# An encoder layer on one core: the last three down projections computed with 128 tokens on the output's partitions, and the Fourier projection's weights placed 192 bytes further in their slots

## The chip, the core and the metric

The kernel runs on one core of one Trainium2 chip. The metric is device time in microseconds for one call, the median of several runs. A profile of one execution goes with it: every instruction of each engine with its start and duration, and every DMA.

The engines are named as in the profile: PE (TensorE, products), PEld (its loading of the stationary operand), DVE (VectorE), ACT (ScalarE), POOL (GpSimd) and SP, which issues most DMAs.

## The reference

One layer of an encoder on 512 tokens with 1024 features, all in fp32:

```python
def reference(x, ...):
    x = x + 0.5 * swiglu(rms_norm(x, ffn1_norm), ffn1_w_gate, ffn1_w_up, ffn1_w_down)
    h = rms_norm(x, mix_norm)
    u = h @ w_in
    f_out = fourier_mixer(u[..., :o0], fnet_w, fnet_b)       # 512 columns
    a_out = gqa_attention(u[..., o0:o1], u[..., o1:o2], u[..., o2:], q_norm, k_norm)
    x = x + jnp.concatenate([f_out, a_out], axis=-1) @ w_out
    x = x + 0.5 * swiglu(rms_norm(x, ffn2_norm), ffn2_w_gate, ffn2_w_up, ffn2_w_down)
    return rms_norm(x, final_norm)

def swiglu(h, w_gate, w_up, w_down):
    return (jax.nn.silu(h @ w_gate) * (h @ w_up)) @ w_down
def rms_norm(x, g):
    return x * lax.rsqrt(jnp.mean(x * x, axis=-1, keepdims=True) + EPS) * g
```

The hidden width of the two feed-forward parts is 2752: 21 blocks of 128 and a tail of 64.

## The kernel before

The state `x` lies transposed: eight blocks `x[k]` (k = 0 to 7) of 128 features on the partitions and 512 tokens along the free axis. Every operand of a product is split into a high and a low part (fp32r), and each product is made as three: high weights with high data, high weights with low data, low weights with high data (`product`, lines 160 to 163).

**The ring.** `ring` holds twelve slots of 4096 bytes per partition. The first eight (`own`) hold the scaled state in high and low parts (`hh`, `hl`) while a projection reads it, and otherwise weights; the other four (`plain`, slots 8 to 11, in pairs of a high and a low one) hold weights. Between the large tiles stand small unused ones (`room`), which set how far apart the addresses of a product's two operands are. SKIP puts the weights of the last three down projections 64 bytes further in their slots.

**Feed-forward.** The 21 hidden blocks go in groups, the last of them 14 to 20. In a group, `seven` makes the gate and up projections of each block by a scheme of seven half-size products (L389, 256 columns, tiles p, q and r), and `down` adds the group's share of the down projection to each of the eight feature blocks (L160 to L163, tile dn, 512 columns). `rest` is the piece of `seven` that stands behind the first of these. The first products of such a run are cut in two (CUT).

**The mixers** run by an order written out by hand (ORDER). There the Fourier projection (`fproject_ops`, L940 to L942) makes 8 blocks of 24 products with 256 columns: the scaled state in the ring is the stationary operand, the weights f0 to f3, in pairs of plain slots or in the tile `more`, are the moving one.

**The end.** In the second feed-forward part the last three feature blocks (5, 6, 7) are left to `closing`. It scales the first five blocks by the final gain (`gained`), then makes the three down projections for tokens 0 to 255, block after block, and then again for tokens 256 to 511. Each adds to the state (`residual`, L476), is squared (`square`, L194) and added to the sum of squares `acc`. In the middle of the second half the norm of the first half is worked out (`column`: sums over the partitions by products with ones, L216; `mean`, L223; `power`, L230, on POOL), turned into a row (`turn`, L235) and multiplied on the first half's output (`finish`, L1282 on DVE and L1278 on POOL), which goes out. After the last product the same follows for tokens 256 to 511. `awake` makes products without use, so that PE is not idle meanwhile.

PE and SP execute in the order of the program in both feed-forward parts. There, DVE, ACT and POOL get an order by what is ready first, worked out when the program is built.

Of the kernel before, what the change touches and what calls it, by code (L numbers as in the profile page):

```python
# [13 lines left out]
P = 128  # L14
S = 512
# [6 lines left out]
HD = 64  # L22
EPS = 1e-6
WARM = 9
NS = 12

GROUPS1 = ((0, "t", 1, 2), range(3, 9), range(9, 15), range(15, 21))
# [47 lines left out]
def asf(ap):  # L75
    return ap.bitcast(F32)
# [3 lines left out]
def encoder(ctx, tc, A, out):  # L80
    nc = tc.nc
    cp = ctx.enter_context(tc.tile_pool(name="const", bufs=1))
    wp = ctx.enter_context(tc.tile_pool(name="weights", bufs=3))
    ring = cp.tile([P, NS, KD * P], F32R, name="ring")
    taken = []

    def room(pool, n):
# [10 lines left out]
    def bank(name):  # L98
        return pp.tile([P, S], F32, tag="bank", name=name)
# [6 lines left out]
    hh = [ring[:, k, 0:S] for k in range(KD)]  # L106
    hl = [ring[:, k, S:] for k in range(KD)]


    def in_order():  # L110
# [6 lines left out]
    def lows(lo, src, hi):  # L117
        nc.vector.tensor_tensor(out=lo, in0=src, in1=asf(hi), op=ALU.subtract)  # L118

    slots = [ring[:, i, :] for i in range(NS)]  # L120
    plain = slots[KD:]

    def slot():
# [22 lines left out]
    def weights(src, name, n=KD, raw=None, by_dma=False, skip=0):  # L146
        raw = raw or raw_tile(src, name, n)
        hi, lo = weight_slots(n, skip)
        if name in HI_DVE:
            nc.vector.tensor_copy(hi[:, :n, :], raw[:, :n, :])  # L150
        else:
            nc.scalar.copy(hi[:, :n, :], raw[:, :n, :])  # L152
# [103 lines left out]
    def ffn(norm, after, wgu, wd, wdt, groups, opening, closing):  # L256
# [6 lines left out]
        with tc.tile_pool(name=f"act{n_}", bufs=1) as ap, tc.tile_pool(name=f"sums{n_}", bufs=2) as sp:  # L263
# [4 lines left out]
            wt = []  # L268
            free, where = list(range(PLACES)), {}

            def place(j):
# [1 line left out]
                return where[j]  # L273

            own, shared = slots[:KD], slots[KD:]

            def gate(c, between={}, by_dma=False):
                whi, wlo = weights(wgu[c], f"gu{n_}_{c}", by_dma=by_dma)
# [175 lines left out]
            def down(d, group, gi):  # L454

                js = [j for j in group if j != "t"]
                whi, wlo = weights(wd[d][:, js[0] : js[-1] + 1, :], f"dn{n_}_{d}_{gi}", len(js), skip=SKIP if closing and gi == len(groups) - 1 and d >= KD - 3 else 0)
                w = wt[d // 4][:, d % 4 * P : (d % 4 + 1) * P]

                def steps(ps, t):  # L460
                    for i, j in enumerate(group):
                        h, l = (at[:, where[j], o, t] for o in range(2))
                        first, last = i == 0, i == len(group) - 1
                        if j == "t":
                            nc.tensor.matmul(ps[:, t], w, h, start=first, stop=False)
                            nc.tensor.matmul(ps[:, t], w, l, start=False, stop=last)
                        else:
                            k = j - js[0]
                            cut = first and d == KD - 3 and t == slice(0, HALF)
# [3 lines left out]
                return steps  # L473

            def residual(d, ps, t):
                nc.vector.scalar_tensor_tensor(  # L476
# [4 lines left out]
            for gi, group in enumerate(groups):  # L481
# [34 lines left out]

                waiting, downs = [], []
                for d in range(KD):
                    if last and closing and d == KD - 3:
                        closing([(e, down(e, group, gi)) for e in range(d, KD)], residual)  # L520
# [24 lines left out]
                    waiting = []  # L545
# [133 lines left out]
    with tc.tile_pool(name="mix", bufs=1) as mp, tc.tile_pool(name="mixt", bufs=1) as mt:  # L679

        room(mp, 192)
        more = mp.tile([P, 2, KD * P], F32R, name="more")
        more = [more[:, i, :] for i in range(2)]
        plain.extend(more)

        def temp(name):
# [40 lines left out]
        def weight_ops(name, src, n=KD):  # L727
            @op(f"{name}.r")
            def _():
                raws[name] = raw_tile(src, name, n)  # L730

            @op(f"{name}.h")
            def _():
                ws[name] = hi, lo = tuple(weight_slots())
                (nc.vector.tensor_copy if name in HI_DVE else nc.scalar.copy)(hi[:, :n, :], raws[name][:, :n, :])
# [531 lines left out]

    by_pool = (2, 3)

    def finish(c0, c1, row, parts):  # L1270

        t = slice(c0 * P, c1 * P)
        pr = row(c0, c1)
        for ks in parts:
            block = slice(ks[0], ks[-1] + 1)
            if ks[0] in by_pool:
                for k in ks:
                    nc.gpsimd.tensor_tensor(out=x[k][:, t], in0=x[k][:, t], in1=n3.rb[:, t], op=ALU.mult)  # L1278
                    nc.scalar.dma_start(out=out[:, k, t], in_=x[k][:, t])
            else:  # L1280
                y = xt[:, block, t]
                nc.vector.tensor_tensor(out=y, in0=y, in1=pr[:, t].unsqueeze(1).to_broadcast(list(y.shape)), op=ALU.mult)  # L1282
                nc.sync.dma_start(out=out[:, block, t], in_=y)

    def gained(k, t=slice(0, S)):
        nc.scalar.activation(x[k][:, t], x[k][:, t], AF.Copy, scale=gains[:, 3, k : k + 1])
# [5 lines left out]
        for _ in range(2 * n):  # L1292
            nc.tensor.matmul(ps[:, : 2 * P], unit[:, :P], unit, start=True, stop=True)

    def closing(downs, residual):

        for k in range(downs[0][0]):
            gained(k)
        t0, t1 = slice(0, S // 2), slice(S // 2, S)

        def more(sq, t):
            nc.vector.tensor_tensor(out=n3.acc[:, t], in0=n3.acc[:, t], in1=sq[:, t], op=ALU.add)

        for d, steps in downs:
            ps = bank(f"last{d}0")
            for _ in steps(ps, t0):
                pass
            residual(d, ps, t0)
            more(n3.square(d, t0), t0)
            gained(d, t0)  # L1310
        i = 0
        for d, steps in downs:
            ps = bank(f"last{d}1")
            for _ in steps(ps, t1):
                i += 1
                if i == 5:
                    n3.column([n3.acc], 0, 2)
                if i == 9:
                    finish(0, 2, n3.row, ((0, 1), (4, 5), (2, 3), (6, 7)))
            if d < KD - 1:  # L1320
                residual(d, ps, t1)
                sq = n3.square(d, t1)
                if d == downs[0][0]:
                    more(sq, t1)
                gained(d, t1)

        pc = bank("ss3_2")
        for c in (2, 3):
            n3.sum(pc, c, [n3.acc], first=c == 2, last=False, skip_group_check=True)
        awake(1)  # L1330
        for c in (2, 3):
            n3.sum(pc, c, [sq], first=False, last=False, skip_group_check=True)
        residual(KD - 1, ps, t1)
        sq = n3.square(KD - 1, t1)
        gained(KD - 1, t1)
        for c in (2, 3):
            n3.sum(pc, c, [sq], first=False, last=c == 3, skip_group_check=True)
        awake(2)
        n3.mean(pc, 2, 4)
        n3.power(2, 4)  # L1340
        finish(2, 4, n3.rows, ((0,), (1,), (4, 5), (2, 3), (6, 7)))
# [50 lines left out]
def _layout(i):  # L1392
# [13 lines left out]
    def down(w):  # L1406
# [27 lines left out]
        "wdt1": i["ffn1_w_down"][NF * P :],  # L1434
        "wdt2": i["ffn2_w_down"][NF * P :],
        "wins": chunks(w_in[:, np.concatenate([k, q, v])]),
        "winf": w_in[:, :512].reshape(2, 4, P, 2, 256).transpose(3, 0, 2, 1, 4).reshape(4, P, 4, 256),
        "wo": chunks(i["w_out"][mix]),
    }
# [21 lines left out]
```

## Time and profile before

| what | value |
|---|---|
| median of 3 runs | 841.4 us (841.1 to 841.55) |
| the profiled execution | 841.31 us, span 839.5 us |
| PE busy | 831.3 us, 5433 products |
| DVE, ACT, POOL busy | 637.6, 463.7, 31.7 us |
| DMA | 84.0 MB read, 2.1 MB written |

The span is the time from the first to the last instruction that the profiler records; the rest of the execution's time lies around it. Products are pipelined: what a product costs is the distance between its start and the next one's start, not its own duration. In a row of the timeline stand the start, the duration, the engine, the line, the operation and the tiles (output, arrow, inputs), the shape and the count. In a row of the groups stand the count, the busy time and the mean duration in ns, and behind the next bar the idle time ahead of the group with the engine that ended it.

### The profile page before, as it was taken

How to read it: one execution, taken by the hardware profiler on the slowest of the kernel's cores; microseconds unless marked ns; L12 is line 12 of the kernel's file. 1: busy time of each engine (PE TensorE's matmuls, PEld its weight loads, DVE VectorE, ACT ScalarE, POOL GpSimd, SP SyncE). 2: the span in 40 equal slices, each digit the busy share in tenths (PEclk: the TensorE clock that was granted, in tenths of full speed). 3: DMA queues.
4: the chain of work that ended last, by engine and by line, in shares of the span. 5: the costliest groups of instructions: out<-in, count | busy, mean ns of one | idle time of the engine just before them, and what ended most of it. 6: DMA issues, size and time to landing. Idle time of an engine off the chain costs nothing.

```text
span 839.5 us, 13715 instructions
## 1 busy us (share of the span) xinstructions
PE 831.3 (99%) x5433; PEld 753.4 (90%) x5433; DVE 637.6 (76%) x1003; ACT 463.7 (55%) x777; POOL 31.7 (4%) x35
## 2 busy tenths in 40 slices
PE   9999999999999999999999999999999999999996
PEld 6888998899989998889998888899988998899986
DVE  6998896489746847699998388999945896489553
ACT  7763664167424744677776357656632673167452
POOL 0110000000000000221000000100000000000002
PEclk9999999999999999999999999999999999999999
DMA  7664322323242213522020224543233322323213
GB/s 251 171 149 164 126 89 76 119 101 138 77 137 101 70 47 112 189 84 75 26 76 26 85 90 114 119 160 118 93 117 110 133 89 77 119 101 100 70 58 101
DMA packets 31568, 89.38 MB, mean 106 GB/s; under 512 B 3728, under 2 KB 9360, under 8 KB 31504
## 3 DMA queue, kind: packets, MB, share of 16 engines
q1 hardware_dynamic: 28320, 82.87, 29.3%
q0 software_dynamic: 2608, 5.12, 3.3%
q8 instruction: 42, 0.69, 0.3%
q10 hardware_dynamic: 576, 0.52, 0.2%
q14 instruction: 22, 0.18, 0.1%
HBM read 84.04 MB, written 2.10 MB: 103 GB/s over the span
## 4 chain that ended last, share of the span: by engine, by line
PE 99%; POOL 0%; issue 0%; POOLq 0%; DVE 0%
PE r L389 23%; PE q L389 11%; PE dn L160 9%; PE dn L163 9%; PE dn L162 9%; PE p L389 6%; PE mix L160 3%; PE mix L162 3%; PE mix L163 3%; PE gu L640 3%; PE gu L160 3%; PE gu L163 3%; PE gu L162 3%; PE mix L1145 2%; PE mix L1102 2%; PE mix L1076 1%
## 5 line engine op out<-in xcount | busy, mean ns | idle before, releaser
L389 PE MATMUL r<-rt,ring 128*128 128x256 f32 x1686 | 209.7, 276 | 0.0
L389 PEld LDWEIGHTS r<-rt,ring 128*128 128x128 f32 x1686 | 200.7, 188 | 0.9
L162 PE MATMUL dn<-at,ring 128*128 128x512 f32 x300 | 116.7, 389 | 0.0
L163 PE MATMUL dn<-at,ring 128*128 128x512 f32 x300 | 116.7, 389 | 0.0
L160 PE MATMUL dn<-at,ring 128*128 128x512 f32 x300 | 116.7, 389 | 0.0
L389 PE MATMUL q<-rt,ring 128*128 128x256 f32 x840 | 106.7, 276 | 0.0
L118 DVE TENSOR_TENSOR ring<-s,ring 128x1024 fp32r<-128x1024 f32 x70 | 85.5, 1221 | 24.3 <-ACT ring L348 20.9
L476 DVE SCALAR_TENSOR_TENSOR gx<-dn,gx 128x512 f32<-128x512 f32 x61 | 42.0, 689 | 80.6 <-PE dn L163 80.6
L389 PEld LDWEIGHTS q<-rt,ring 128*128 128x128 f32 x840 | 100.5, 188 | 0.0
L152 ACT CAST ring<-raw_dn 128x768 fp32r<-128x768 f32 (+3 forms) x58 | 45.5, 788 | 82.9 <-PE dn L162 74.7
L348 ACT CAST ring<-s 128x1024 fp32r<-128x1024 f32 x70 | 73.5, 1050 | 28.7 <-PE p L389 15.0
L163 PEld LDWEIGHTS dn<-at,ring 128*128 128x128 f32 x300 | 56.3, 188 | 11.8
L162 PEld LDWEIGHTS dn<-at,ring 128*128 128x128 f32 x300 | 56.3, 188 | 11.3
L160 PEld LDWEIGHTS dn<-at,ring 128*128 128x128 f32 x300 | 56.3, 188 | 11.2
L118 DVE TENSOR_TENSOR ring<-raw_dn,ring 128x768 fp32r<-128x768 f32 (+3 forms) x58 | 51.6, 892 | 5.9 <-PE r L389 4.6
L389 PE MATMUL p<-rt,ring 128*128 128x256 f32 x420 | 53.3, 276 | 0.0
L118 DVE TENSOR_TENSOR ring<-raw_g,ring 128x1024 fp32r<-128x1024 f32 x35 | 42.7, 1219 | 10.3 <-PE p L389 10.3
L389 PEld LDWEIGHTS p<-rt,ring 128*128 128x128 f32 x420 | 50.2, 188 | 0.0
L348 ACT CAST ring<-raw_g 128x1024 fp32r<-128x1024 f32 x35 | 36.8, 1052 | 14.5 <-DMA raw_g<-in_wgu 8.8
L397 ACT COPY p<-r 128x256 f32<-128x256 f32 x35 | 12.9, 369 | 49.0 <-PE r L389 48.7
L421 ACT ACTIVATE g<-g 128x512 f32<-128x512 f32 x35 | 22.2, 633 | 23.4 <-DVE g L420 23.2
L357 ACT CAST ring<-raw_u 128x512 fp32r<-128x512 f32 x35 | 21.8, 624 | 17.0 <-PE q L389 16.2
(307 smaller groups left out, 1570.4 us busy)
## 6 DMA issues: line engine op xcount, KB each, us to landing
raw_g<-in_wgu SPq DMA_DIRECT2D x35, 512.0 KB, 3.6
raw_u<-in_wgu SPq DMA_DIRECT2D x35, 512.0 KB, 4.3
raw_dn<-in_wd SPq DMA_DIRECT2D x40, 384.0 KB, 3.1
raw_gu<-in_wgu SPq DMA_DIRECT2D x12, 512.0 KB, 3.6
raw_o<-in_wo SPq DMA_DIRECT2D x8, 512.0 KB, 3.5
raw_dn<-in_wd SPq DMA_DIRECT2D x8, 448.0 KB, 3.2
raw_wq<-in_wins SPq DMA_DIRECT2D x4, 512.0 KB, 4.4
raw_f<-in_winf SPq DMA_DIRECT2D x4, 512.0 KB, 4.0
```

The costliest lines, as they stand in the source:

```text
L118: nc.vector.tensor_tensor(out=lo, in0=src, in1=asf(hi), op=ALU.subtract)
L152: nc.scalar.copy(hi[:, :n, :], raw[:, :n, :])
L160: nc.tensor.matmul(ps, whi, mhi, start=first, stop=False)
L162: nc.tensor.matmul(ps[:, t], whi, mlo[:, t], start=False, stop=False)
L163: nc.tensor.matmul(ps, wlo, mhi, start=False, stop=last)
L348: nc.scalar.copy(hi, src)
L357: nc.scalar.copy(hi, src)
L389: nc.tensor.matmul(ps[:, t], a[:, ks], b[:, i, t], start=first and i == 0 and o == 0, stop=i == KH - 1 and o == 2, skip_group_check=not first,
L421: nc.scalar.activation(b["g"], b["g"], AF.Silu)
L476: nc.vector.scalar_tensor_tensor(out=x[d][:, t], in0=ps[:, t], scalar=0.5, in1=x[d][:, t], op0=ALU.mult, op1=ALU.add)
L640: nc.tensor.matmul(pss[c], w[:, k % 2, c], m[k], start=k == 0 and m is hh and w is hi, stop=k == KD - 1 and w is lo,)
L1102: nc.tensor.transpose(pts[n][:, c * P : (c + 1) * P], prob[t, b, c][:, kc * P : (kc + 1) * P], ident)
```

## The change

**The end.** The products of tokens 0 to 255 stay. For tokens 256 to 511, the three blocks of features are no longer made one after the other. `token_weights` makes a second copy of the three down projections' weights, times 0.5, in two tiles `tw` (high and low) laid out as 384 features beside each other, in slots 0 to 5. `by_tokens` then takes 128 tokens at a time: it turns the state's three blocks into the bank by three transposes, and adds 21 products with the hidden data as the stationary operand and 384 feature columns as the moving one. The bank holds tokens on the partitions, state already included, so the residual, its square and its gain are not separate steps. `inverse` squares the bank with a sum along the free axis and adds it to the rest of the mean square. `finish` scales these 384 features by the token's factor and a broadcast gain row `gt`, loaded from memory, and the other five blocks by the turned row, and sends 128 tokens out at a time. The first of the two groups of tokens is finished while the second is made, after 12 of its 21 products.

**The output's layout** changes to one piece for each half, put in order on the host.

**The mixers.** The pairs of slots that hold f0 to f3 are used 192 bytes (48 elements) further (`further`). For that, 256 bytes are left between slots 9 and 10 and behind slot 11, and behind the second slot of `more`. Slots 10 and 11 stand 256 bytes further in the whole kernel.

```diff
+FURTHER = 48
+FURTHER_IN = "f0", "f1", "f2", "f3"
+ROOM = 64
+LAST = 3
...
-    ring = cp.tile([P, NS, KD * P], F32R, name="ring")
+    ring = cp.tile([P, NS * KD * P + 2 * ROOM], F32R, name="ring")
...
-    slots = [ring[:, i, :] for i in range(NS)]
+    def slot_at(tile, i, rooms=0):
+        o = i * KD * P + rooms * ROOM
+        return tile[:, o : o + KD * P]
+
+    slots = [slot_at(ring, i, int(i >= KD + 2)) for i in range(NS)]
+
+    def further(tile, i, rooms=0):
+        o = i * KD * P + rooms * ROOM + FURTHER
+        return tuple(tile[:, o + j * KD * P : o + (j + 1) * KD * P].rearrange("p (a b) -> p a b", b=P) for j in range(2))
...
+            def token_weights(d, group):
+                c = slice((d - KD + LAST) * P, (d - KD + LAST + 1) * P)
+                hi, lo = (t[:, : len(group), c] for t in tw)
+                raw = raws[d][:, : len(group)]
+                nc.scalar.activation(hi, raw, AF.Copy, scale=0.5)
+                nc.vector.scalar_tensor_tensor(
+                    out=lo, in0=raw, scalar=0.5, in1=asf(hi), op0=ALU.mult, op1=ALU.subtract
+                )
+
+            def by_tokens(ps, c, group):
+                t = slice(c * P, (c + 1) * P)
+                for i in range(LAST):
+                    nc.tensor.matmul(
+                        ps[:, i * P : (i + 1) * P], x[KD - LAST + i][:, t], ident, is_transpose=True,
+                        start=i == 0, stop=False, skip_group_check=True,
+                    )
+                for j in group:
+                    h, l = (at[:, where[j], o, t] for o in range(2))
+                    whi, wlo = (w[:, j - group[0]] for w in tw)
+                    for a, b in ((h, whi), (l, whi), (h, wlo)):
+                        nc.tensor.matmul(
+                            ps[:, : LAST * P], a, b, start=False, stop=j == group[-1] and b is wlo, skip_group_check=True
+                        )
+                    yield
...
-    def closing(downs, residual):
+    def closing(downs, residual, by_tokens, finished):
...
+        gt = tp.tile([P, S], F32, tag="wide", bufs=1, name="gt")[:, :n]
+        nc.sync.dma_start(out=gt, in_=A["gt"])
...
+        def inverse(c, ps, z=None):
+            sq = tp.tile([P, S], F32, tag="sq", name=f"sqt{c}")
+            cs = slice(c, c + 1)
+            nc.scalar.activation(sq[:, :n], ps[:, :n], AF.Square, scale=D**-0.5, accum_out=squares[:, cs])
+            if c == 3:
+                sums = bank("ss3_3")
+                n3.sum(sums, c, [n3.acc])
+                n3.mean(sums, c, c + 1)
+            nc.vector.tensor_tensor(out=squares[:, cs], in0=squares[:, cs], in1=n3.ms[:, cs], op=ALU.add)
+            nc.gpsimd.tensor_tensor(out=n3.r[:, cs], in0=squares[:, cs], in1=mhalf[:, cs], op=ALU.pow)
+            if c == 3:
+                nc.vector.tensor_tensor(out=z, in0=ps[:, :n], in1=gt, op=ALU.mult)
+
+        def finish(c, ps, last):
+            t = slice(c * P, (c + 1) * P)
+            pr = bank(f"rp3_{c}")
+            n3.turn(pr, c)
+            y = finished(c)
+            r = n3.r[:, c : c + 1]
+            if last:
+                nc.scalar.activation(y[:, :n], z, AF.Copy, scale=r)
+                nc.scalar.dma_start(out=rest[:, c - 2, :n], in_=y[:, :n])
+            else:
+                nc.vector.scalar_tensor_tensor(out=y[:, :n], in0=ps[:, :n], scalar=r, in1=gt, op0=ALU.mult, op1=ALU.mult)
+            for a, b, how in ((0, 3, nc.sync), (3, fewer, nc.scalar)) if last else ((0, fewer, nc.sync),):
+                o = y[:, n + a * P : n + b * P]
+                row = pr[:, t].unsqueeze(1).to_broadcast([P, b - a, P])
+                nc.vector.tensor_tensor(out=o.rearrange("p (k s) -> p k s", s=P), in0=xt[:, a:b, t], in1=row, op=ALU.mult)
...
+        for c in (2, 3):
+            ps = bank(f"last{c}")
+            for i, _ in enumerate(by_tokens(ps, c)):
+                if (c, i) == (2, 2):
                     n3.column([n3.acc], 0, 2)
+                    sums = bank("ss3_2")
+                    n3.sum(sums, 2, [n3.acc])
+                    n3.mean(sums, 2, 3)
+                if (c, i) == (2, 5):
+                    finish_half()
+                if (c, i) == (3, 3):
+                    finish(*done[-1], False)
+            inverse(c, ps, z)
+            done.append((c, ps))
+        awake(4)
+        finish(*done[-1], True)
```

More of the change, by code (lines that the diff above doesn't have):

```diff
@@ L105, in encoder @@
     x = [xt[:, k, :] for k in range(KD)]
-    hh = [ring[:, k, 0:S] for k in range(KD)]
-    hl = [ring[:, k, S:] for k in range(KD)]
+    hh = [ring[:, k * KD * P : k * KD * P + S] for k in range(KD)]
+    hl = [ring[:, k * KD * P + S : (k + 1) * KD * P] for k in range(KD)]
     def in_order():
@@ L275, in ffn @@
             own, shared = slots[:KD], slots[KD:]
+            tw = [
+                ring[:, 3 * i * KD * P : 3 * i * KD * P + PLACES * LAST * P]
+                .rearrange("p (m c) -> p m c", c=LAST * P) for i in range(2)
+            ]
             def gate(c, between={}, by_dma=False):
@@ L456, in down @@
                 js = [j for j in group if j != "t"]
-                whi, wlo = weights(wd[d][:, js[0] : js[-1] + 1, :], f"dn{n_}_{d}_{gi}", len(js), skip=SKIP if closing and gi == len(groups) - 1 and d >= KD - 3 else 0)
+                src, halves_ = wd[d][:, js[0] : js[-1] + 1, :], closing and gi == len(groups) - 1 and d >= KD - LAST
+                raw = raws[d] = raw_tile(src, f"dn{n_}_{d}_{gi}", len(js))
+                whi, wlo = weights(src, "", len(js), raw, skip=SKIP if halves_ else 0)
+                if halves_:
+                    token_weights(d, js)
                 w = wt[d // 4][:, d % 4 * P : (d % 4 + 1) * P]
@@ L518, in ffn @@
                 for d in range(KD):
-                    if last and closing and d == KD - 3:
-                        closing([(e, down(e, group, gi)) for e in range(d, KD)], residual)
+                    if last and closing and d == KD - LAST:
+                        closing(
+                            [(e, down(e, group, gi)) for e in range(d, KD)], residual,
+                            lambda ps, c: by_tokens(ps, c, group), finished,
+                        )
                         break
@@ L681, in encoder @@
         room(mp, 192)
-        more = mp.tile([P, 2, KD * P], F32R, name="more")
-        more = [more[:, i, :] for i in range(2)]
+        more_tile = mp.tile([P, 2 * KD * P + ROOM], F32R, name="more")
+        more = [slot_at(more_tile, i) for i in range(2)]
         plain.extend(more)
@@ L734, in _ @@
                 ws[name] = hi, lo = tuple(weight_slots())
+                if name in FURTHER_IN:
+                    i = next(i for i, t in enumerate([slots[KD], slots[KD + 2], more[0]]) if t is plain[-2])
+                    assert plain[-1] is [slots[KD + 1], slots[KD + 3], more[1]][i]
+                    ws[name] = hi, lo = further(*((ring, KD, 0), (ring, KD + 2, 1), (more_tile, 0))[i])
                 (nc.vector.tensor_copy if name in HI_DVE else nc.scalar.copy)(hi[:, :n, :], raws[name][:, :n, :])
@@ L1268, in encoder, with finish_half @@
     by_pool = (2, 3)
[L1270 to L1275, printed above, removed]
+    first, rest = out[0].rearrange("p (k s) -> p k s", s=HALF), out[1].rearrange("p (c n) -> p c n", n=D)
+    def finish_half():
+        t = slice(0, HALF)
+        pr = n3.row(0, 2)
+        for ks in (0, 1), (4, 5), (2, 3), (6, 7):
             if ks[0] in by_pool:
@@ L1293, in awake @@
             nc.tensor.matmul(ps[:, : 2 * P], unit[:, :P], unit, start=True, stop=True)
-    def closing(downs, residual):
-        for k in range(downs[0][0]):
+    def closing(downs, residual, by_tokens, finished):
+        n, fewer = LAST * P, KD - LAST
+        gt = tp.tile([P, S], F32, tag="wide", bufs=1, name="gt")[:, :n]
+        nc.sync.dma_start(out=gt, in_=A["gt"])
+        for k in range(fewer):
             gained(k)
-        t0, t1 = slice(0, S // 2), slice(S // 2, S)
-        def more(sq, t):
-            nc.vector.tensor_tensor(out=n3.acc[:, t], in0=n3.acc[:, t], in1=sq[:, t], op=ALU.add)
+        t0 = slice(0, HALF)
         for d, steps in downs:
@@ L1308, in closing @@
             residual(d, ps, t0)
-            more(n3.square(d, t0), t0)
+            sq = n3.square(d, t0)
+            nc.vector.tensor_tensor(out=n3.acc[:, t0], in0=n3.acc[:, t0], in1=sq[:, t0], op=ALU.add)
             gained(d, t0)
[L1311 to L1316, printed above, removed]
-                    n3.column([n3.acc], 0, 2)
[L1318 to L1339, printed above, removed]
@@ new lines, in finish @@
+        def finish(c, ps, last):
[13 more added lines that the diff above has]
+                nc.vector.tensor_tensor(out=o.rearrange("p (k s) -> p k s", s=P), in0=xt[:, a:b, t], in1=row, op=ALU.mult)
+                o = o if last else y
+                how.dma_start(out=rest[:, c - 2, n + a * P : n + b * P] if last else rest[:, c - 2], in_=o)
```

26 lines of the change are left out of this document (18 added, 8 removed).

## The prediction

> **What bounds the kernel now.** I read the page first: its busy line and the chain that ended last.
>
> ```profile
> span 839.5 us, 13715 instructions
> ...
> PE 831.3 (99%) x5433; PEld 753.4 (90%) x5433; DVE 637.6 (76%) x1003; ACT 463.7 (55%) x777; POOL 31.7 (4%) x35
> ...
> PE 99%; POOL 0%; issue 0%; POOLq 0%; DVE 0%
> ```
>
> TensorE is the bound until its last product, so two things can move the time: the pitch at which products start, and the piece behind the last product. The profiled execution took 841.31 us for a span of 839.5, so 1.8 us lie around the span; the median of the runs is 841.4. I sum in the span and carry the difference to 841.4. A change of 0.2%, 1.7 us, is about what a measurement can tell from none.
>
> Next the timeline of the end, whose rows carry the sum:
>
> ```profile
> 821.49 0.28 PE L160 MATMUL last<-at,ring 128*128 128x256 f32 x1
> ...
> 823.08 0.28 PE L163 MATMUL last<-at,ring 128*128 128x256 f32 x1
> 823.20 0.50 PE L216 MATMUL ss<-ones,acc 128*128 128x2 f32 x4
> ...
> 823.76 0.28 PE L162 MATMUL last<-at,ring 128*128 128x256 f32 x1
> ...
> 825.05 0.38 PE L235 MATMUL rp<-ident,r 128*128 128x128 f32 x2
> ...
> 825.39 0.28 PE L162 MATMUL last<-at,ring 128*128 128x256 f32 x1
> ...
> 829.39 0.28 PE L163 MATMUL last<-at,ring 128*128 128x256 f32 x1
> 829.51 0.51 PE L216 MATMUL ss<-ones,acc 128*128 128x2 f32 x4
> 829.71 0.43 DVE L476 SCALAR_TENSOR_TENSOR gx<-last,gx 128x256 f32<-128x256 f32 x1 [1.62 <-PE last L163]
> 830.17 0.42 ACT L194 ACTIVATE sq<-gx 128x256 f32<-128x256 f32 x1 [1.08 <-DVE gx L476]
> 831.28 0.16 DVE L223 TENSOR_SCALAR ms<-ss 128x2 f32<-128x2 f32 x1 [1.15 <-PE ss L216]
> 831.52 0.69 POOL L230 TENSOR_TENSOR r<-ms,mhalf 128x2 f32<-128x2 f32 x1 [4.17 <-DVE ms L223]
> 832.28 0.65 PE L235 MATMUL rp<-ident,r 128*128 128x128 f32 x4 [0.57 <-POOL r L230]
> 832.74 1.95 DVE L1282 TENSOR_TENSOR gx<-gx,rp 128x256 f32<-128x256 f32 x4 [1.30 <-PE rp L235]
> 833.19 0.34 SPq L1283 DMA_DIRECT2D out_y<-gx  x1
> 834.17 1.03 ACTq L1279 DMA_DIRECT2D out_y<-gx  x2
> ```
>
> The second half of the tokens begins on TensorE at 821.49 and its 63 products end at 829.51: 8.02 us. Behind them lie 9.99 us: 2.71 until the power ends (832.21), then scaling and output. The DMA view from 833.2 to 838.2 (slices of 0.125 us) shows the output:
>
> ```profile
> GB/s 0 0 0 0 0 0 57 319 336 271 140 328 336 238 123 311 336 344 336 262 352 385 344 336 320 336 352 352 352 344 352 344 320 156 8 0 0 0 0 0
> ```
>
> Bytes start at 833.95, 0.8 us behind the first issue at 833.19, and flow without a gap until 837.5: 1.05 MB at 300 GB/s. The span ends 2.0 us after them. So the end is set by when the last megabyte starts and by its size.
>
> **Pitch of the new products.** The change replaces 63 products of 256 columns by 42 of 384 (two times 128 tokens, seven blocks, three products), with six transposes of x ahead of them. No row has 384 columns. Neighbours:
>
> ```profile
> 801.07 0.39 PE L163 MATMUL dn<-at,ring 128*128 128x512 f32 x1
> ...
> 804.47 0.39 PE L163 MATMUL dn<-at,ring 128*128 128x512 f32 x1
> ...
> 785.07 1.36 PE r L389 x12
> ...
> 793.24 1.41 PE r L389 x12
> ...
> 409.35 1.03 PE L1102 MATMUL mix<-ident,e 128*128 128x128 f32 x8
> 410.14 0.48 PE L1076 MATMUL mix<-ks,qb 128*128 128x512 f32 x1
> ```
>
> Fifteen products of 512 columns take 3.40 us, 0.227 each. Products of 256 columns have two pitches: 0.113 in a long run (1.36 for 12), 0.118 after an interruption (1.41 for 12; and 34 from 825.39 to 829.39 in 4.00). Per column 512 is as fast as the quick 256. So 384 costs 0.170 to 0.177; I take 0.172, nearest to the 512 row, since a weight load has more time to hide. 42 × 0.172 = 7.2 us (7.1 to 7.4).
>
> The interruptions: four records of sums cost 823.76 − 823.20 less one product of 0.12, 0.44 us; two turns cost 825.39 − 825.05 less one product, 0.22; eight transposes take 0.79, about 0.10 each, and the switch back 0.08. New in this stage: two groups of three transposes (0.77), six records of sums instead of four (0.65), two turns (0.22), one turn (0.13): 1.8 us. Together 9.0 against 8.02: the last product ends 1.0 us later, at 830.5.
>
> ```profile
> L1102 PE MATMUL mix<-ident,e 128*128 128x128 f32 x128 | 17.7, 272 | 0.0
> ```
>
> The same transposes last 272 ns each here. The Trainium skill ("TensorE: Matmul & The Clock Gate", Part 4: PE-mode transpose) gives about 275 ns for one in a kernel, which agrees as a duration; taken as the price of each, six would cost 1.65 us and the whole change would come out near 840.5. The pitch of 0.10 in the eight above says otherwise.
>
> **Behind the last product.** Removed: residual, the sums over the last square, four of the turns, and half of the final scaling and output. New chain: Square of 384 columns with an accumulator straight from the bank, an add, the power, one turn, two DVE multiplies (384 and 256) beside one ACT copy of 384, three DMAs of 0.52 MB together.
>
> ```profile
> L1090 ACT ACTIVATE e<-mix,mx,sc 128x512 f32<-128x512 f32 x32 | 24.9, 782 | 4.3 <-DVE mx L1083 4.0
> ...
> L1090 ACT ACTIVATION_READ_ACCUMULATOR e<-mix,mx,sc 128x1 f32 x32 | 6.4, 199 | 0.0
> ...
> L1286 ACT ACTIVATE gx<-gx 128x512 f32<-128x512 f32 x5 | 3.5, 718 | 0.1
> ...
> L1286 ACT ACTIVATE gx<-gx 128x256 f32<-128x256 f32 x6 | 3.1, 510 | 0.2
> ```
>
> 256 more columns cost ACT 0.21 us (718 against 510). So the Square of 384 is 0.42 + 0.10 = 0.52, at most 0.67 by the accumulating row (782 less 0.10). From the last product: 0.20 until ACT starts (as 829.71 − 829.51), 0.55, 0.20 to read the accumulator, 0.03 and 0.16 for the add (as L223), 0.08, and 0.70 for the power (L230): 1.92 instead of 2.71. The power ends at 832.45, not 832.21.
>
> Then the ACT copy (0.61) puts out its first DMA 0.70 behind the power; the turn and the first DVE multiply put out the second at about 1.0, the third at 1.35. Bytes start 0.8 behind the first issue, and 0.52 MB at 300 GB/s need 1.75: they end 3.25 behind the power, at 835.7. Before it was 837.5, so the span ends 1.8 us earlier: 837.7. If the shorter queue ran at the view's best slices, 350 GB/s, 0.25 more would go; with the slow pitch and the longer Square 0.4 would come back.
>
> **Hidden work.** The 128-token weights need three more ACT casts and three more DVE subtractions of 896 elements:
>
> ```profile
> L152 ACT CAST ring<-raw_dn 128x896 fp32r<-128x896 f32 x8 | 7.5, 944 | 8.9 <-PE dn L162 8.5 <-PE r L389 0.4
> ...
> L118 DVE TENSOR_TENSOR ring<-raw_dn,ring 128x896 fp32r<-128x896 f32 x8 | 8.6, 1091 | 5.6 <-PE r L389 4.6 <-ACT ring L152 0.9
> ...
> 805.00:821.00 16.00, 16.00 (x102) 14.40 (x101) 8.76 (x13) 8.43 (x13) 0.00 (x0) 1.00 0.05 19
> ```
>
> That is 2.8 us on ACT and 3.3 on DVE, in 16 us in which they are busy 8.4 and 8.8 under the downs; nothing waits for them before 821.5. They wait for the slots that the twelve products at 793.24 read last, long done. Without that cover up to 3.3 us would be paid. The gain row's DMA goes out on SP behind the last weights, long before any output. The scaling of tokens 256 to 383 and its 0.52 MB run under the last group's products, and the multiply by the gain under the last power. Wider rows on the way out (2 to 4 KB) I cost at nothing, since the bytes flow at 300 GB/s with 1 KB rows already.
>
> **The Fourier projection.** Its 192 products of 256 columns:
>
> ```profile
> 406.13 0.28 PE L941 MATMUL mix<-ring 128*128 128x256 f32 x1
> ...
> 408.77 0.28 PE L942 MATMUL mix<-ring 128*128 128x256 f32 x1
> ```
>
> 22 products take 2.64 us: 0.120, slower than either pitch above. Weights in the slots and activations in the ring both lie at multiples of 512 bytes from one another here; where products of this width run at 0.113 or 0.118 the paddings in the code (`room`, SKIP) put the operands 64 or 192 bytes off such a multiple. Shifted by 192 bytes I expect the interrupted pitch, 0.118, and the first products of a block are quicker than 0.120 already: 192 × 0.0017 = 0.3 us. Bounds: 0 and, at 0.113, 192 × 0.0067 = 1.3. A write of high parts now also waits for the last reader of the neighbouring slot, one product later: nothing.
>
> The sum: −1.8 − 0.3, and 0.1 for a short wait in the next paragraph: −2.0, so 839.4; I write 839.5.
>
> **Rivals.** First, a new wait on TensorE. The turn of tokens 256 to 383 stands 12 products into the last group, about 828.7, and needs Square, add and power of that group, whose products end near 826.4.
>
> ```profile
> 825.92 1.44 POOL L1278 TENSOR_TENSOR gx<-gx,rb 128x256 f32<-128x256 f32 x2 [1.23 <-ACT rb L243]
> ...
> 826.70 1.03 ACTq L1279 DMA_DIRECT2D out_y<-gx  x2
> ```
>
> In between ACT issues two DMAs that wait for POOL's two products, 0.7 apart, and POOL's power comes behind those. If the Square goes ahead of the DMAs, the power ends near 828.85: a wait of 0.1. If ACT holds it behind them (to 828.3), the power ends near 829.95 and TensorE stands 1.3 us: 840.8. For it: ACT is in order. Against: the schedule lets ready work pass.
>
> Second, the shift does nothing for the pitch: 839.8. The Trainium skill ("SBUF — State Buffer", Who interferes with whom) says that PE never waits on anyone for a port; by that rule the 192 bytes buy nothing. The 0.120 beside the 0.113 of the same shape speaks against it.
>
> Third, slower. Slots 10 and 11 move by 256 bytes for the whole kernel, and the products of the seven-product blocks read their weights there too:
>
> ```profile
> L389 PE MATMUL r<-rt,ring 128*128 128x256 f32 x1674 | 209.4, 276 | 0.0
> ...
> L389 PE MATMUL q<-rt,ring 128*128 128x256 f32 x840 | 106.7, 276 | 0.0
> ```
>
> These 2,514 products run at 0.113; the row at 793.24 shows that 0.118 is one interruption away and lasts. If a move between a shifted and an unshifted slot drops them to 0.118, each costs 0.0045 us: 440 products eat the whole gain, and half of them, 1,260, give +5.7, 845. Against it: the remainder against 256 bytes stays the same, and the last downs, whose weights stand 64 bytes further by SKIP, hold 0.113 all the same (14 starts from 821.49 to 823.08 in 1.59).
>
> **Numbers.** Forecast 0.60, 839.5, of its own 838.7 to 840.2; of it 0.48 are faster by over 0.2% (below 839.7) and 0.12 within. New wait 0.15 (840.8): 0.11 within, 0.04 slower, should it also meet the slow pitch. Shift without effect 0.12 (839.8): 0.04 faster, 0.08 within. Slots 10 and 11: 0.08, slower. Fourier at 0.113: 0.05, 838.4, faster. That makes faster 0.57, same 0.31, slower 0.12. The range takes in all but the slots and the rest of the new wait: 838.4 to 841.2.
>
> **What would show it.** Last product ending at 830.5 with products of 384 columns 0.172 apart; the power 1.9 us behind it; bytes ending 1.8 us earlier than before; Fourier products 0.118 apart; r and q at 276 ns and no TensorE wait for POOL at the turn. Wrong: a wait there over 0.5 us, 0.118 in the long runs, or a last product after 831.

## The result and the profile after

The changed kernel takes 838.7 us (median of 8 runs, 838.24 to 839.23) where the kernel before takes 841.11 (840.59 to 841.55) beside it: ratio 0.9973, 95% interval 0.9965 to 0.9982. It is faster, by 2.4 us; 839.5 had been forecast, in a range of 838.4 to 841.2. The profiled execution took 839.23 us for a span of 837.4.

The page of the profile after, head and chain that ended last:

```profile
span 837.4 us, 13673 instructions
PE 831.0 (99%) x5410; PEld 752.4 (90%) x5410; DVE 639.9 (76%) x1006; ACT 465.2 (56%) x778; POOL 30.7 (4%) x34
...
PE 98%; issue 0%; DMA 0%; DVE 0%; ACT 0%; POOLq 0%; POOL 0%; SPq 0%; DVEq 0%
```

TensorE is as much the bound as before. So the two places to look at are again the pace of its products and the end. The timeline of the end, from the first product of the closing on:

```profile
814.04 0.28 PE L173 MATMUL last<-at,ring 128*128 128x256 f32 x1
...
821.32 0.49 PE L511 MATMUL last<-ident,gx 128*128 128x128 f32 x3
...
826.20 0.49 PE L511 MATMUL last<-ident,gx 128*128 128x128 f32 x3
826.45 2.33 PE L519 MATMUL last<-ring,at 128*128 128x384 f32 x12
...
826.28 1.88 DVE L1344 TENSOR_TENSOR gx<-gx,rp 128x512 f32<-128x512 f32 x3 [2.14 <-ACT rb L256]
826.46 0.49 ACT L1379 ACTIVATE sqt<-last 128x384 f32<-128x384 f32 x1 [0.21 <-PE last L519]
827.10 1.04 ACTq L1340 DMA_DIRECT2D out_y<-gx  x2
828.08 0.15 DVE L1384 TENSOR_TENSOR squares<-squares,ms 128x1 f32<-128x1 f32 x1
828.31 0.55 POOL L1385 TENSOR_TENSOR r<-squares,mhalf 128x1 f32<-128x1 f32 x1 [0.54 <-DVE squares L1384]
828.92 0.32 PE L248 MATMUL rp<-ident,r 128*128 128x128 f32 x1
828.99 1.83 PE L519 MATMUL last<-ring,at 128*128 128x384 f32 x9
830.66 0.28 PE L229 MATMUL ss<-ones,acc 128*128 128x2 f32 x2
830.86 0.49 ACT L1379 ACTIVATE sqt<-last 128x384 f32<-128x384 f32 x1 [3.82 <-PE last L519]
831.72 0.56 POOL L1385 TENSOR_TENSOR r<-squares,mhalf 128x1 f32<-128x1 f32 x1 [2.86 <-DVE squares L1384]
832.95 0.34 ACTq L1397 DMA_DIRECT2D out_y<-y  x1
833.61 0.34 ACTq L1405 DMA_DIRECT2D out_y<-y  x1
```

Read it from the front: the second half of the tokens starts on TensorE at 821.32 and its last product ends at 830.66, 9.34 us. The last power ends at 832.28, 1.6 behind. Three DMAs go out from 832.95 to 833.61. The DMA view from 833 to 836 (slices of 0.075 us) shows their bytes:

```profile
GB/s 0 0 0 0 0 0 0 0 0 0 123 287 307 369 369 410 328 430 328 410 328 389 328 410 342 314 335 314 396 301 151 28 0 0 0 0 0 0 0 0
```

They flow from 833.75 to 835.35: 0.52 MB in 1.6 us, 330 GB/s. Against before, from the start of the second half to the span's end (18.01 us before, 16.08 after):

| piece, us | before | predicted | after |
|---|---|---|---|
| second half's start to last product's end | 8.02 | 9.1 with the wait | 9.34 |
| to the end of the power | 2.70 | 1.92 | 1.61 |
| to the first bytes | 1.74 | 1.50 | 1.48 |
| bytes flow | 3.55 | 1.75 | 1.60 |
| to the span's end | 2.0 | 2.0 | 2.05 |

That is −1.9. The rest lies ahead of the closing. From the first product of the gate and up projections (next two fences, 5.06 after and 4.68 before) to the first of the closing are 808.98 us after (814.04 − 5.06) and 809.53 before (814.21 − 4.68): −0.55. That first product came 0.38 us later in this execution, so the span alone hides part of it.

```profile
5.06 1.22 PE L695 MATMUL gu<-ring 128*128 128x512 f32 x2
```

```profile
4.68 1.65 PE L640 MATMUL gu<-ring 128*128 128x512 f32 x3
```

The Fourier projection is what got quicker. Two of its blocks of 24 products, first and last product of each, in the timeline after:

```profile
410.87 0.28 PE L1000 MATMUL mix<-more,ring 128*128 128x256 f32 x1
...
413.48 0.28 PE L1002 MATMUL mix<-ring 128*128 128x256 f32 x1
...
417.66 0.28 PE L1000 MATMUL mix<-more,ring 128*128 128x256 f32 x1
...
420.37 0.28 PE L1002 MATMUL mix<-ring 128*128 128x256 f32 x1
```

23 steps take 2.61 us in the first block, 0.1135 each, and 2.71 in the second, 0.118. Before, the three blocks that ran without a break lay at 0.119 to 0.120. Here is the first of the two above, 2.74 us:

```profile
410.69 0.28 PE L940 MATMUL mix<-more,ring 128*128 128x256 f32 x1
...
413.43 0.28 PE L942 MATMUL mix<-ring 128*128 128x256 f32 x1
```

From the start of the first Fourier product to the start of the last are 51.90 us before (381.44 to 433.34) and 51.29 after (381.91 to 433.20). The 0.61 us between the two cover the whole 0.55.

The products that use slots 10 and 11 kept their pace. Their mean duration of 276 ns, the same before and after, doesn't show it: the Fourier products above last 0.28 at every pace. The distances between starts do. The chain after, from 783 to 797, has these rows of twelve products:

```profile
784.89 1.36 PE r L407 x12
...
793.07 1.41 PE r L407 x12
```

Before they are 1.36 (785.07) and 1.41 (793.24). Over all starts of such products that follow one another (tiles p, q and r) the mean distance is 113.6 ns in both profiles.

### The profile page after: what moved, and what is told of

Read it like the earlier page. It is cut to its first block, busy times and chain, and to the rows that moved or that the text cites. A ratio compares the mean times of both kernels' runs of the same rounds, so it can differ in the third digit from the quotient of the medians.

```text
span 837.4 us, 13673 instructions
## 1 busy us (share of the span) xinstructions
PE 831.0 (99%) x5410; PEld 752.4 (90%) x5410; DVE 639.9 (76%) x1006; ACT 465.2 (56%) x778; POOL 30.7 (4%) x34
## 4 chain that ended last, share of the span: by engine, by line
PE 98%; issue 0%; DMA 0%; DVE 0%; ACT 0%; POOLq 0%; POOL 0%; SPq 0%; DVEq 0%
PE r L407 23%; PE q L407 11%; PE dn L173 9%; PE dn L176 9%; PE dn L175 9%; PE p L407 6%; PE mix L173 3%; PE mix L175 3%; PE mix L176 3%; PE gu L695 3%; PE gu L173 3%; PE gu L176 3%; PE gu L175 3%; PE mix L1205 2%; PE mix L1162 2%; PE mix L1136 1%
## 5 line engine op out<-in xcount | busy, mean ns | idle before, releaser
L173 PEld LDWEIGHTS dn<-at,ring 128*128 128x128 f32 x300 | 56.3, 188 | 11.2
```

The source lines that it names most:

```text
L173: nc.tensor.matmul(ps, whi, mhi, start=first, stop=False)
```

## The experiments

The two columns on the right of this table come from each run's own profile: from the first product of the gate and up projections to the first product of the closing (the body), and from there to the span's end (the end). They don't contain the moment at which that first product starts, which moves by some tenths between executions (4.57 to 5.40). The span is read to a tenth, so the end is good to 0.05. Ratios are to the kernel before, with 95% intervals; kernels with one run have none.

| kernel | median us | ratio | body us | end us |
|---|---|---|---|---|
| before | 841.11 | | 809.53 | 25.29 |
| changed | 838.7 | 0.9973 [0.9965, 0.9982] | 808.98 | 23.36 |
| changed, once more | 838.81 | 0.9968 [0.9956, 0.9981] | 808.79 | 23.38 |
| end alone | 839.23 | 0.9978 [0.9969, 0.9987] | 809.30 | 23.40 |
| shift alone | 840.6 | 0.9995 [0.9987, 1.0004] | 809.14 | 25.32 |
| shift alone, once more | 841.12 (one run) | | 808.64 | 25.26 |
| shift by 256 bytes | 839.46 | 0.9979 [0.9969, 0.9989] | 809.66 | 23.35 |
| shift by 64 bytes | 838.68 (one run) | | 808.80 | 23.42 |
| transposes twice | 838.98 | 0.9975 [0.9965, 0.9985] | 809.00 | 23.68 |
| bytes late | 839.96 | 0.9986 [0.9977, 0.9995] | 809.01 | 24.47 |
| token weights twice | 838.96 (one run) | | 809.10 | 23.35 |
| turn later | 838.3 | 0.9968 [0.9956, 0.9981] | 809.03 | 23.05 |
| turn later, once more | 838.16 | 0.9961 [0.9947, 0.9974] | 808.72 | 23.01 |
| two multiplies | 837.77 (one run) | | 808.28 | 22.99 |

**The end alone and the shift alone.**

```diff
-FURTHER_IN = "f0", "f1", "f2", "f3"
-ROOM = 64
+FURTHER_IN = ()
+ROOM = 0
```

> The change without its shift: slots, rings and Fourier weights where the kernel before had them, the end by 128 tokens kept. Theory: the profile of the changed kernel gives 1.9 us of the gain to the end and 0.6 to the Fourier projection, so this kernel takes 0.6 us more than the changed one (839.3) and 1.8 less than the one before; its Fourier products lie 0.120 apart. Rival (the shift has no effect, the rest of the gain came with the end): 838.7, as the changed kernel. Rival (the shift did most): 840.5 or more.

For the shift alone, `FURTHER`, `ROOM`, `slot_at`, `further` and their uses went into the kernel before.

> The kernel before with the shift alone: end by 256 tokens. Theory: 840.5, 0.6 less than before; Fourier blocks at 0.113 or 0.118 between starts where it was 0.120, r and q still 276 ns. Rival (no effect): 841.1. Rival (slots 10 and 11 hurt r and q): over 842.

The end alone takes 1.7 us off (839.23 against 840.95 beside it), near what its profile has: 25.29 to 23.40. The shift alone gives 0.35 us by the medians, which the interval doesn't tell from nothing, and −0.39 in the body. Its end is that of the kernel before. The two parts act apart from one another. But its three unbroken Fourier blocks of 24 products all lay at 0.118, where two of the changed kernel's three ran at 0.1135 for all or most of their steps, at the same addresses. So it was profiled once more:

> The kernel before with the shift alone, once more, for its profile: in the first one all Fourier blocks lay at 0.118, in three kernels with the new end two blocks of 24 lay at 0.114, with the same addresses. If the pace of a block is chosen anew in each execution, the blocks here can differ from the first profile; if it is fixed by the program, all lie at 0.118 again.

Timeline of the shift alone, first profile, then second, the block that begins on `more`:

```profile
410.61 0.28 PE L956 MATMUL mix<-more,ring 128*128 128x256 f32 x1
...
413.31 0.28 PE L958 MATMUL mix<-ring 128*128 128x256 f32 x1
```

```profile
410.97 0.28 PE L956 MATMUL mix<-more,ring 128*128 128x256 f32 x1
...
413.58 0.28 PE L958 MATMUL mix<-ring 128*128 128x256 f32 x1
```

2.70 us in the first, 2.61 in the second: the same program took a block at 0.118 and at 0.1135. ("All Fourier blocks" in the expectation holds for the blocks of 24 alone. In the first profile, too, some of the runs of 12 were at 0.1135, such as the one from 385.58.) So the program and its addresses don't fix this pace. The two profiles are from two chips. But the two profiles of the later turn, further down, are from one chip and differ as well, by less: the twelve products from 398.25 in the one come to 0.1135 after two steps, the same twelve, from 397.85, in the other after five. What decides it stays open. The second profile's time, 841.12, is no shorter than the 841.05 of the kernel before beside it; its first product of the gate and up projections starts at 5.40, where it is 4.68 in the profile before.

Over the three kernels without an effective shift the body takes 809.50 on average (809.53, 809.30, 809.66), over the other eleven profiles 808.86 (808.28 to 809.14), and the two groups don't overlap. That is −0.64. Nearly all of it lies in the Fourier projection: from its first product to its last are 51.90 to 51.93 us in the three and 51.29 to 51.49 in the eleven, −0.57 on average. The granted clock is 1.00 from 375 to 436 us in all fourteen profiles, so the clock doesn't make the difference.

**Which distance counts.** `FURTHER = 64` (256 bytes) and `FURTHER = 16` (64 bytes) instead of 48:

> The changed kernel with the Fourier weights 256 bytes further instead of 192 (slots 10 and 11 stay 256 bytes further too). Theory (what counts is the remainder of the distance between activations and weights against 256 bytes): the shift then does nothing, the Fourier products are 0.120 apart again and the kernel takes 839.2, as with the end alone. Rival (any place off the common multiple of 512 bytes will do): 0.114 to 0.118 apart, 838.7.

> The changed kernel with the Fourier weights 64 bytes further instead of 192. Theory (remainder against 256 bytes, any but zero): Fourier products 0.114 or 0.118 apart as in the changed kernel, closing begins at about 814.0. Rival (192 bytes in particular, or the larger distance): 0.120.

Timeline, the same block, of the shift by 256 and then by 64 bytes:

```profile
410.79 0.28 PE L1000 MATMUL mix<-more,ring 128*128 128x256 f32 x1
...
413.54 0.28 PE L1002 MATMUL mix<-ring 128*128 128x256 f32 x1
```

```profile
410.41 0.28 PE L1000 MATMUL mix<-more,ring 128*128 128x256 f32 x1
...
413.02 0.28 PE L1002 MATMUL mix<-ring 128*128 128x256 f32 x1
```

2.75 against 2.61 us. At 256 bytes all of the shift's gain is gone: the body is that of the unshifted kernels and the time, 839.46, that of the end alone. At 64 bytes it is there, in the body; its time is a single run. So a larger distance alone doesn't help, and neither does the move of slots 10 and 11, which all three kernels share. The theory's remainder against 256 bytes fits. But a remainder against 128 bytes fits as well, since 64 and 192 bytes leave the same one, 64. A shift by 128 bytes would tell the two apart; it wasn't run.

**What a transpose costs.**

```diff
-                for i in range(LAST):
+                for i in 2 * [*range(LAST)]:
```

> The changed kernel with each group of three transposes of x into the bank written twice, the second over the first. Theory (they cost their pitch, 0.10 to 0.11): the stage is 0.65 us longer, 839.35. Rival (each costs its full duration of 275 ns): 1.65 us longer, 840.35. Part of it could go into the existing wait at the turn, 0.35 us, only if the second group were late there; it isn't, since the wait starts from that group's own end.

Timeline of the second half with them:

```profile
820.90 0.82 PE L511 MATMUL last<-ident,gx 128*128 128x128 f32 x6
...
826.70 2.33 PE L519 MATMUL last<-ring,at 128*128 128x384 f32 x12
...
828.87 0.29 PE L248 MATMUL rp<-ident,r 128*128 128x128 f32 x1
828.92 1.83 PE L519 MATMUL last<-ring,at 128*128 128x384 f32 x9
830.58 0.28 PE L229 MATMUL ss<-ones,acc 128*128 128x2 f32 x2
```

In the row of six, 0.82 instead of 0.49: three more take 0.33 us, 0.11 each, and not 275 ns. The stage is 9.68 us, 0.34 longer, and the end 0.31. Here the last sentence of the expectation is wrong: I had put the second group of transposes behind the start of the wait. They stand between the end of the first group's products, from which the wait counts, and the turn. So their 0.33 us went into the wait: the turn follows its twelve products at 828.87 at once. Only the first group's 0.33 us are paid.

**The output's bytes.** The 0.52 MB of tokens 256 to 383 leave last, on SP's queue, instead of under the last products:

```diff
-                how.dma_start(out=rest[:, c - 2, n + a * P : n + b * P] if last else rest[:, c - 2], in_=o)
+                if last:
+                    how.dma_start(out=rest[:, c - 2, n + a * P : n + b * P], in_=o)
+            early.append(y)
+            if last:
+                nc.sync.dma_start(out=rest[:, 0], in_=early[0])
...
-        done = []
+        done, early = [], []
```

> The changed kernel with one DMA moved: the 0.52 MB of tokens 256 to 383 go out behind the last tokens' rows instead of under the last products; all arithmetic stays. Theory (the end is set by the start and the size of the last bytes): 0.52 MB at 350 GB/s, so the bytes and the span end 1.4 us later than in the changed kernel, 840.1. Rival (the end is the last issue and a fixed latency): 0.3 later, 839.0.

DMA view from 832.5 to 838.5 (slices of 0.15 us):

```profile
GB/s 0 0 0 0 0 0 184 348 348 379 359 379 358 359 338 328 526 410 437 410 355 410 382 437 246 0 0 0 0 0 0 0 0 0 0 0 0 0 0 0
DMA packets 576, 1.05 MB, mean 175 GB/s; under 512 B 64, under 2 KB 448, under 8 KB 576
```

The bytes flow 2.85 us (833.4 to 836.25) instead of 1.6, the end is 1.1 us longer (24.47 against 23.36), and the ratio lies 0.0013 to 0.0018 above the changed kernel's two, 1.1 to 1.5 us. The last issue stood 1.40 us behind its power here and 1.33 in the changed kernel, so it isn't the issue but the size of the last output that sets the end. The 1.4 us expected were somewhat too many for the profile: 350 GB/s had been taken for the 0.52 MB, and all 1.05 MB together went at 370 (300 in the kernel before).

**The wait at the turn.** In the profile after, the turn comes 2.47 us behind the first of its twelve products (826.45 to 828.92). The power that it waits for ends at 828.86. In the row of the doubled transposes the same twelve take 2.17 (826.70 to 828.87), so TensorE stood for 0.3. Two ways were tried to be rid of it. First, the turn three products later:

```diff
-                if (c, i) == (3, 3):
+                if (c, i) == (3, 4):
```

> The changed kernel with the turn of tokens 256 to 383 three products later in the last group. Theory: TensorE's wait there, 0.35 us in the profile, goes, and nothing behind it is late (the scaling of those tokens would end near 831.0, ahead of the last add at 831.5): 0.3 us less than the changed kernel, 838.4. Rival (the wait is no loss, or DVE's scaling now delays the last add): 838.7 to 839.0.

Then both kernels on one chip:

> The changed kernel itself once more, beside the one with the later turn on the same chip: 838.7, stage of 9.3 us with a wait of 0.35 at the turn. The Fourier blocks of 24 products may lie at 0.114 or 0.118 in another order than in its first profile.

> The turn three products later, on the same chip as the changed kernel: 0.35 less than that, 838.35, stage of 9.0 us. Rival (the first difference was the chip's): no difference.

Timeline of the later turn, second run:

```profile
820.58 0.49 PE L511 MATMUL last<-ident,gx 128*128 128x128 f32 x3
...
825.70 2.85 PE L519 MATMUL last<-ring,at 128*128 128x384 f32 x15
827.56 0.55 POOL L1385 TENSOR_TENSOR r<-squares,mhalf 128x1 f32<-128x1 f32 x1 [0.56 <-DVE squares L1384]
828.39 0.27 PE L248 MATMUL rp<-ident,r 128*128 128x128 f32 x1
...
829.56 0.28 PE L229 MATMUL ss<-ones,acc 128*128 128x2 f32 x2
```

The power ends at 828.11, the turn comes at 828.39 behind its products, and the stage is 8.98 us where it was 9.34. The end is 0.31 to 0.37 us shorter than the changed kernel's. The median lies 0.4 below it in the first comparison and 0.65 on the same chip, with runs that don't overlap (837.85 to 838.37 against 838.38 to 839.06). Of the 0.65 the pair's profiles place 0.37 in the end and 0.07 in the body. The other 0.2 is not the edit's: the first product of the gate and up projections starts at 4.83 in the one and at 4.57 in the other. This version is faster than both kernels.

Second, what made the power late. VectorE's third multiply of the first half left out:

```diff
-                nc.vector.tensor_tensor(out=y, in0=y, in1=pr[:, t].unsqueeze(1).to_broadcast(list(y.shape)), op=ALU.mult)
+                if ks[0] != 6:
+                    nc.vector.tensor_tensor(out=y, in0=y, in1=pr[:, t].unsqueeze(1).to_broadcast(list(y.shape)), op=ALU.mult)
```

> The changed kernel without VectorE's third scaling multiply of the first half (channels of blocks 6 and 7 go out unscaled; their DMA stays). Theory (the power of tokens 256 to 383 is late because its add stands behind three multiplies on VectorE): the add comes 0.63 earlier, the power starts when POOL's own products end (827.8) and ends at 828.35, TensorE doesn't wait at the turn, stage of 9.0 us. Rival (ScalarE's square or POOL's queue sets the power): power still ends 828.85 and the wait stays.

Its timeline (the lines after the edit stand one further):

```profile
820.19 0.49 PE L511 MATMUL last<-ident,gx 128*128 128x128 f32 x3
...
825.15 1.29 DVE L1345 TENSOR_TENSOR gx<-gx,rp 128x512 f32<-128x512 f32 x2 [2.14 <-ACT rb L256]
...
825.19 1.44 POOL L1339 TENSOR_TENSOR gx<-gx,rb 128x256 f32<-128x256 f32 x2 [1.60 <-ACT rb L256]
...
826.35 0.30 DVE L1385 TENSOR_TENSOR squares<-squares,ms 128x1 f32<-128x1 f32 x1
...
826.73 0.55 POOL L1386 TENSOR_TENSOR r<-squares,mhalf 128x1 f32<-128x1 f32 x1
...
827.48 0.27 PE L248 MATMUL rp<-ident,r 128*128 128x128 f32 x1
...
829.18 0.28 PE L229 MATMUL ss<-ones,acc 128*128 128x2 f32 x2
```

The add comes when VectorE is through with two multiplies, the power ends at 827.28, and the turn follows its twelve products, 2.17 us behind the first, with no wait: stage 8.99 us, end 22.99. So the wait came from VectorE's queue. POOL's own products end at 826.63 here, just ahead of the power, so the power could not have come much earlier. The single time, 837.77, isn't the value of this: the body was the shortest of all as well.

**The cover of the token weights.** `token_weights(d, js)` is called twice.

> The changed kernel with the weights for the products by tokens written twice (three more ScalarE activations and three more VectorE operations of 896 elements under the downs). Theory (they lie under TensorE's products): closing as long as before, 23.4 us from its first product to the span's end, 838.7. Rival (the cover is nearly used up): up to 3 us longer.

Busy time of the engines from 805 to 821 in it:

```profile
805.00:821.00 16.00, 16.00 (x104) 14.48 (x103) 12.93 (x18) 11.23 (x17) 0.00 (x0) 1.00 0.16 56
```

VectorE is busy 12.9 of 16 us, ScalarE 11.2, and TensorE all of it. The end is 23.35, as without. The cover holds, with room left for about one more such copy on VectorE.

## Why the prediction was right

The forecast's case came true: faster, with the end giving most of it. By its steps:

- **Pitch of 384 columns**, 0.172 taken: 0.1735 in every run of products not interrupted. Interruptions, 1.8: the stage without its wait is 8.98 and 8.99 us in the two kernels that don't wait, 9.0 predicted. 42 products at 0.1735 are 7.3, so the interruptions cost 1.7. The transposes, taken at a pitch of 0.10, cost 0.11 each. The Trainium skill ("TensorE: Matmul & The Clock Gate", Part 4: PE-mode transpose) gives about 275 ns for one in a kernel. The trace agrees with that as the duration of one (0.27), but it isn't the price.
- **The wait at the turn**, 0.1 taken: 0.3 to 0.36 (9.34 less 8.98). This term was mis-sized. The order on ScalarE was judged rightly: the Square ran at 826.46, ahead of the DMAs at 827.10, so the rival at 840.8 didn't come. Counted from the stage's start, the power was expected to end at 7.36 us (828.85 − 821.49) and ended at 7.54 (828.86 − 821.32). The working had named POOL's own products as what holds it, and left out the add on VectorE, which stood behind three multiplies until 828.08. With two multiplies the power ends at 7.09 (827.28 − 820.19), and the wait is gone.
- **Behind the last product**, 1.92 taken to the power's end: 1.61. Too long by 0.14 at the power, which took 0.56 with one column instead of the 0.69 of two columns in the row it was taken from; the rest is in the Square, 0.39 to its sum's reading and not 0.55. First bytes as forecast.
- **Bytes**, 300 GB/s taken: 330, and 370 in the run with the bytes late. In that run the same 1.05 MB went in 576 packets, before in 1120. That the wider rows, which the prediction costed at nothing, make the difference fits this, but it wasn't tried alone.
- **The Fourier projection**, 0.3 taken within 0 and 1.3: 0.64. The direction and the place were right, the size was off because the products do not stay at 0.118 but run at 0.1135 in part of each execution. The rival at 839.8, a shift without effect, falls: with the same instructions the body is 809.50 us without an effective shift and 808.86 with it. The Trainium skill ("SBUF — State Buffer", Who interferes with whom) says that PE never waits on anyone. The prediction had read this as leaving no room for a gain, and there the measurement decides; whether PE waits at a port in the slower products, no run shows.
- **Slots 10 and 11**: the sign that was named, r and q at 276 ns, came, but as a duration it couldn't have failed: the Fourier products show the same duration at every pace. The distance between starts is 113.6 ns before and after. No kernel with the slots moved has a longer body than the kernel before, but for the one whose Fourier weights stand 256 bytes further, by 0.13. The rival at 845 falls.
- **Hidden weights**: shown hidden, also at twice the work (one run).

The sum was −2.0, of which −1.7 for the end and −0.3 for Fourier. The profile has −1.9 and −0.55 to −0.64. Both gains were put too small, and what was missed at the turn (0.25 too little cost) was less than what was missed behind the last product (0.3 at the power and 0.15 at the bytes, both too much). So the end comes out near its forecast partly by luck: three terms of it were off, and not all the same way. Of the 0.8 us between 839.5 and 838.7, another 0.3 is the kernel before, whose median was 841.4 in the 3 runs that the forecast started from and 841.11 in 8. One of the signs didn't come: TensorE does wait at the turn, though for less than the 0.5 us that were to show the forecast wrong.

## What to carry to other kernels

When products end the kernel, what stands behind the last one can be worth more than the products themselves: here 1.3 us more of them, with the wait, were paid back with 3.3 us by a shorter chain and half the last bytes. When an engine's small operation feeds a step that TensorE waits for, look at what is queued ahead of it on every engine of that chain, and place the step that needs it later if that costs nothing. And where products of one shape have two paces in a trace, compare how far apart their operands' addresses are, and read the pace from the starts, not from the durations.

## What the runs showed of the hardware

- Products of 128 by 128 by 256 columns ran 0.120, 0.118 or 0.1135 us apart with the same instructions, at a granted clock of 1.00 and with the same duration of 0.28 by their rows. With the weights moved by 0 or 256 bytes the unbroken blocks of 24 were at 0.119 to 0.120. Moved by 64 or 192 bytes they were at 0.118 or at 0.1135, with the change from one to the other also inside a block, and this differed between two executions of one program. What chooses between these two stays open.
- The power of one column on POOL took 0.55 to 0.56 us, that of two columns 0.69 to 0.71.
- A transpose costs TensorE 0.11 us when others of its kind stand beside it, though each one lasts 0.27 by its row.
